# Splitting streamed weights with transfers and ScalarE instead of ScalarE and VectorE

## The chip, the cores and the metric

One core of one Trainium2 chip. The kernel is a two-layer decoder trunk on 512 tokens in float32. The metric is the device time of one execution in microseconds (us).

## The reference, cut to what matters

```python
D_MODEL = 1024; SEQ = 512; DEPTH = 2
A_WIDTH = 2048; B_WIDTH = 1536; D_FF = 3072

def mixer_a(h, w_in, v_gain, w_s, b_s, w_out):
    z = jax.nn.gelu(h @ w_in)                    # w_in: 1024 x 4096
    u, v = jnp.split(z, 2, axis=-1)
    v = rms_norm(v, v_gain)
    ...                                          # chunks of 128 tokens, 8 groups
    sv = jnp.einsum("gts,bcsgd->bctgd", ws, v) + ...
    return (u * sv) @ w_out                      # 2048 x 1024

def mixer_b(h, w_in, ...):
    g, xb = jnp.split(h @ w_in, 2, axis=-1)      # 1024 x 3072
    ...                                          # convolution, two gates of 6 x 256 x 256 each, a scan
    return (hs * gelu(g)) @ w_out                # 1536 x 1024

def conv_ffn(h, w_up, conv_w, conv_b, w_down):
    up = causal_dwconv(h @ w_up, conv_w, conv_b) # 1024 x 6144
    gate, val = jnp.split(up, 2, axis=-1)
    return (jax.nn.gelu(gate) * val) @ w_down    # 3072 x 1024

def reference(x, ...):
    for i in range(DEPTH):
        h = rms_norm(x, norm_mix[i])
        x = x + (mixer_a(h, ...) if i % 2 == 0 else mixer_b(h, ...))
        h = rms_norm(x, norm_ffn[i])
        x = x + conv_ffn(h, ...)
    return rms_norm(x, norm_final)
```

All weights are float32 in the chip's memory and are used once per execution.

## The kernel before, in words

**Products.** Activations lie with their features on the partitions and the 512 tokens along the free dimension. To keep float32 accuracy, every operand of a large product is held in two parts of type float32r, a rounded large part and a small part that is the remainder; `mm3` multiplies large by large, large by small and small by large, three matmuls of 512 columns.

**Chunks.** Weights arrive in chunks of 256 input features by 512 output features: 512 KB, 1024 values on each of 128 partitions. There are 230 of them that go through `load`; four more, at the very start, go through `first_chunk`. Each is used for 24 matmuls (2 halves of the input features x 4 blocks of outputs x 3), in the order of the program: `av` and `au` (the two halves of `a_w_in`), `aow` (`a_w_out`), `fu0` (`f_w_up` of layer 0, 12 blocks of 4 chunks), `fd0` (`f_w_down`, 24 chunks), `bx`, `bg` (`b_w_in`) with the six gate chunks `gw` between them, `bow`, `fu1`, `fd1`. The number after the letters is block and chunk: `fu052` is chunk 2 of block 5. The chunks of `f_w_up` take two transfers of 256 KB, one from the gate half and one from the value half; the others take one of 512 KB, and the gate chunks take two.

**The split.** `load` fetches a chunk from SP's queue into a `raw` tile. `split` makes the large part `hi` by a copy on ScalarE (L89) and the small part `lo` by a subtraction on VectorE (L90). The three tags `raw`, `hi`, `lo` of the pool `wp` have three buffers each, so a chunk can be fetched and split well ahead of its matmuls. Both instructions are given a high priority, which the scheduler uses when it writes down each engine's order; after that each engine works strictly through its own queue.

**Other work.** VectorE and ScalarE also scale the products, run the convolutions (`conv`), the activations and the split of the activations (`to_parts`). In mixer A, `gate_spatial` puts small matmuls (`sv`, L418 and L419) between the chunks of `au1` to `aow0`. GpSimd does a handful of small things: the power -1/2 of the norms (`rsqrt_mean`, L213), a mask, one power for the decay constants (L175).

Of the kernel before, what the change touches and what calls it, by code (L numbers as in the profile page):

```python
# [8 lines left out]
F32 = mybir.dt.float32  # L9
BF16 = mybir.dt.bfloat16  # L10
F32R = mybir.dt.float32r
AF = mybir.ActivationFunctionType
ALU = mybir.AluOpType

P = 128
S = 512
# [4 lines left out]
AG = 8  # L21
# [6 lines left out]
HIGH = 1000  # L28
LRU_C = 8.0

# Columns of the packed per-channel vectors.
_COLS = {}
_off = 0
for _name, _n in (
# [10 lines left out]
def trunk(ctx: ExitStack, tc: tile.TileContext, xT, vecs, a_w_in, a_w_sT, a_b_s, a_w_out,  # L45
          b_w_in, b_w_a, b_w_x, b_w_out, f_w_up, f_w_down, out):
    nc = tc.nc

    const = ctx.enter_context(tc.tile_pool(name="const", bufs=1))
    wp = ctx.enter_context(tc.tile_pool(name="wp", bufs=3))  # L50
    yp = ctx.enter_context(tc.tile_pool(name="yp", bufs=24))
    wk = ctx.enter_context(tc.tile_pool(name="wk", bufs=7))
    pp = ctx.enter_context(tc.tile_pool(name="pp", bufs=8, space=bass.MemoryType.PSUM))
# [4 lines left out]
    def work(name="w"):  # L58
        return wk.tile([P, S], F32, tag="w", name=name)
# [4 lines left out]
    def yhi(name="yh"):  # L64
        return yp.tile([P, S], F32R, tag="yh", name=name)
# [1 line left out]
    def ylo(name="yl"):  # L67
        return yp.tile([P, S], F32R, tag="yl", name=name)

    # Activations whose tables differ, in the order of the program.  # L70
    last_act = []

    def act_in_order(*args, **kw):
# [7 lines left out]
    def small(n, name):  # L81
        return const.tile([P, n], F32, name=name)

    # A chunk of a weight: 1024 values a partition, in two parts that add up to it exactly.
    def split(raw, shape, name):
        hi = wp.tile(shape, F32R, tag="hi", name=f"{name}h")
        lo = wp.tile(shape, F32R, tag="lo", name=f"{name}l")
        with tc.high_priority(HIGH):
            nc.scalar.copy(hi, raw)  # L89
            nc.vector.tensor_tensor(lo, raw, hi.bitcast(F32), op=ALU.subtract)  # L90
        return hi, lo

    def load(shape, parts, name):
        raw = wp.tile(shape, F32, tag="raw", name=f"{name}r")
        for sl, src in parts:
            nc.sync.dma_start(sl(raw), src)
        return split(raw, shape, name)

    def mm3(ps, w, x, first, last):
        (wh, wl), (xh, xl) = w, x  # L100
# [1 line left out]
        nc.tensor.matmul(ps, wh, xl, start=False, stop=False)  # L102
        nc.tensor.matmul(ps, wl, xh, start=False, stop=last)  # L103

    # Feature-major product: one PSUM tile for each of four blocks of 128 output features.
    def block(kt, loader, acts, name, hooks={}):
        pss = [psum(f"{name}{m}") for m in range(4)]
        for kc in range(kt // 2):
            hi, lo = loader(kc)
            last = kc == kt // 2 - 1  # L110
            order = [(k, m) for m in range(4) for k in range(2)] if last else [(k, m) for k in range(2) for m in range(4)]
            for k, m in order:
                kk = 2 * kc + k
                w = (hi[:, k, m * P:(m + 1) * P], lo[:, k, m * P:(m + 1) * P])
                mm3(pss[m], w, acts[kk], kk == 0, kk == kt - 1)
            for hook in hooks.get(kc, ()):
                hook()
        return pss

    def loader_of(w, col, name):  # L120
        v = w.rearrange("(k p) n -> p k n", p=P)

        def f(kc):
            return load([P, 2, 512], [(lambda t: t, v[:, 2 * kc:2 * kc + 2, col:col + 512])], f"{name}{kc}")
        return f

# [1 line left out]
    vt = const.tile([P, NV], F32, name="vt")  # L128
    xall = const.tile([P, KD, S], F32, name="xall")
    xs = [xall[:, k, :] for k in range(KD)]  # L130
# [6 lines left out]
    def load_x(k):  # L137
        nc.sync.dma_start(xs[k], xT[k * P:(k + 1) * P, :])

    # Keeps the tensor engine's clock up while the first loads are under way.  # L140
    warm = work("warm").bitcast(BF16)[:, 0:S]
    nc.vector.memset(warm, 0.0)
    wps = psum("warm")
# [13 lines left out]
    mhalf = small(NC, "mhalf")  # L157
    nc.gpsimd.memset(mhalf, -0.5)

    # log of the sigmoid, by log1p(u) = 2 atanh(u / (2 + u)) with u = exp(-|lambda|)  # L160
    lam = vt[:, _COLS["b_lambda"]:_COLS["b_lambda"] + NB]
    ebase = small(NB, "ebase")
    nabs = small(NB, "nabs")
# [1 line left out]
    u = small(NB, "lu")  # L165
# [20 lines left out]
        nc.vector.tensor_scalar(c8, u, -LRU_C, None, op0=ALU.mult)  # L186
        nc.vector.tensor_scalar(c4, u, LRU_C / 2, None, op0=ALU.mult)

# [1 line left out]
    acc = const.tile([P, S], F32, name="acc")  # L190
    rbc = const.tile([P, S], F32, name="rbc")
    rc = small(NC, "rc")
# [4 lines left out]
    def norm_input(k, gain, ts=slice(None)):  # L197
        nc.scalar.activation(xh[k][:, ts], xs[k][:, ts], AF.Copy, scale=gain)  # L198
        nc.vector.scalar_tensor_tensor(  # L199
            xl[k][:, ts], xs[k][:, ts], gain, xh[k][:, ts].bitcast(F32), op0=ALU.mult, op1=ALU.subtract)  # L200
# [11 lines left out]
        nc.vector.tensor_scalar(ms[:, 0:w], total, 1.0 / n, EPS, op0=ALU.mult, op1=ALU.add)  # L212
        nc.gpsimd.tensor_tensor(dst, ms[:, 0:w], mhalf[:, 0:w], op=ALU.pow)  # L213

    # The token's sum over the features, one token a partition.
    def norm_stat():
        ps = psum("st")
        for c in range(NC):
            nc.tensor.matmul(ps[:, c:c + 1], acc[:, c * P:(c + 1) * P], ones_f[:, 0:1], start=True, stop=True)
        rsqrt_mean(rc, ps[:, 0:NC], D)  # L220

    # The same scale along the free dimension, on all partitions.
    def norm_spread():
        nc.vector.tensor_copy(rch, rc)
        nc.vector.tensor_tensor(rcl, rc, rch.bitcast(F32), op=ALU.subtract)
        pb = psum("rb")
        for i, r in enumerate((rch, rcl)):
            dg = work_r("dg")
            nc.vector.tensor_tensor(
                dg.rearrange("p (c t) -> p c t", c=NC),  # L230
                ident.unsqueeze(1).broadcast_to([P, NC, P]),
                r.bitcast(F32).unsqueeze(2).broadcast_to([P, NC, P]), op=ALU.mult)
            nc.tensor.matmul(pb, ones, dg, start=i == 0, stop=i == 1)
        nc.scalar.copy(rbc, pb)
# [6 lines left out]
        nc.vector.tensor_tensor(l, src, h.bitcast(F32), op=ALU.subtract)  # L241
        return h, l

    # A product back to the model's width, added to x; the next norm's input follows.
    def project(kt, w, acts, gain_name, gain_off, name, hooks={}):
        for mb in range(2):
            pss = block(kt, loader_of(w, mb * 512, f"{name}w{mb}"), acts, f"{name}p{mb}", {} if mb else hooks)
            for m in range(4):
                k = 4 * mb + m
                nc.vector.tensor_tensor(xs[k], pss[m], xs[k], op=ALU.add)  # L250
                norm_input(k, col(gain_name, gain_off + k))
                square(k)

    # The last one, with the norm that ends the trunk. The last chunks of the second block go by halves
    # of the tokens, so that the first half leaves while the second is multiplied.
    def project_out(kt, w, acts, name):
        sq7 = work("sq7")
        hw = S // 2
# [67 lines left out]
    nc.vector.memset(tiny, 0.0)  # L326
    nc.scalar.activation(tiny, tiny, AF.Gelu_apprx_tanh)

# [1 line left out]
    vsum = small(NC * 4, "vsum")  # L330
    vparts = {}
    vraw = {}
    wv = a_w_in.rearrange("(k p) n -> p k n", p=P)

    def first_chunk(kc, src):
        raw, hi, lo = (wp.tile([P, 2, 512], dt, tag=t, name=f"av0{kc}{t}") for dt, t in ((F32, "raw"), (F32R, "hi"), (F32R, "lo")))
        for i in range(2):
            k = 2 * kc + i
            load_x(k)
            nc.sync.dma_start(raw[:, i], src[:, i])  # L340
            with tc.high_priority(HIGH):
                norm_input(k, g0[:, k:k + 1])
                nc.scalar.copy(hi[:, i], raw[:, i])
                nc.vector.tensor_tensor(lo[:, i], raw[:, i], hi[:, i].bitcast(F32), op=ALU.subtract)
        return hi, lo

    for fb in range(4):
        pss = [psum(f"v{c}") for c in range(NC)]
        for kc in range(KD // 2):
            c0 = AW + fb * 512  # L350
            if fb == 0:
                hi, lo = first_chunk(kc, wv[:, 2 * kc:2 * kc + 2, c0:c0 + 512])
            else:
                hi, lo = load([P, 2, 512], [(lambda t: t, wv[:, 2 * kc:2 * kc + 2, c0:c0 + 512])], f"av{fb}{kc}")
            if fb == 1 and kc == 2:
                norm_spread()
            last = kc == KD // 2 - 1
            order = [(k, c) for c in range(NC) for k in range(2)] if last else [(k, c) for k in range(2) for c in range(NC)]
# [13 lines left out]
        for c in range(NC):  # L372
            v = yp.tile([P, S], F32, tag="yl", name=f"vr{c}{fb}")
            nc.scalar.activation(v, pss[c], AF.Gelu_apprx_tanh, scale=rc[:, c:c + 1])
            junk = work("junk")
            i = c * 4 + fb
# [6 lines left out]
    for fb in range(4):  # L383
        for c in range(NC):
            v, sc = vraw[c, fb], rv[:, c:c + 1]
# [2 lines left out]
            nc.vector.scalar_tensor_tensor(l, v, sc, h.bitcast(F32), op0=ALU.mult, op1=ALU.subtract)  # L388
            vparts[c, fb] = (h, l)

    # The lower triangle of the spatial weights, [s, g, t]: s <= t stays.
    wsr = wp.tile([P, AG, P], F32, tag="raw", name="wsr")
    nc.sync.dma_start(wsr, a_w_sT.rearrange("g s t -> s g t"))
    wsparts = []
    for i in range(AG // 2):
# [4 lines left out]
        both = yhi(f"ws{i}").rearrange("p (g two t) -> p g two t", g=2, two=2)  # L400
# [4 lines left out]
    yparts = []  # L405
    uts = []

    # v's large part meets both parts of the weights side by side; the small products share one place.
    def gate_spatial(d):
        g = d // 2  # L410
        w = wsparts[g // 2][:, g % 2]
# [26 lines left out]
            uts.append(ut)  # L438
    project(AW // P, a_w_out, yparts, "norm_ffn", 0, "ao", spatial_hooks(3))

# [1 line left out]
    def conv(dst, src, taps, wname, cname, woff, wstep, coff):  # L442
        last = taps - 1
        nc.scalar.activation(dst, src, AF.Identity, scale=col(wname, woff + last * wstep), bias=col(cname, coff))  # L444
        for i in range(1, taps):
            nc.vector.scalar_tensor_tensor(  # L446
                dst[:, i:], src[:, :S - i], col(wname, woff + (last - i) * wstep), dst[:, i:],
                op0=ALU.mult, op1=ALU.add)
# [31 lines left out]
    conv_ffn(0, "norm_mix", KD)  # L480
    log_sigmoid()

# [1 line left out]
    xbparts = []  # L484
    gts = []

# [21 lines left out]
    rts, ths, its, hss = [], [], [], []  # L508

    gw = {}  # L510

    # r, tanh(-log_a / 2) and i * xb
    def gates(j):
        head, e = j // 2, j % 2
        if not e:
# [112 lines left out]
```

## Time and profile before

| | |
|---|---|
| median of 2 runs | 1341.85 us (1341.41 to 1342.29) |
| profiled execution, first to last instruction (span) | 1339.3 us |
| TensorE (PE) busy | 1329.0 us, 99% |
| VectorE (DVE) busy | 802.6 us, 60% |
| ScalarE (ACT) busy | 554.0 us, 41% |
| GpSimd (POOL) busy | 12.0 us, 1% |
| moved by transfers | 129.19 MB, mean 96 GB/s |

The profile records one execution. It gives no time of its own for that execution beside the span; the timed runs are 2.1 to 3.0 us longer than it, which is what lies around the first and the last instruction. A busy share is an average over stages, and matmuls are pipelined, so a busy PE says that matmuls followed each other closely and not that each ran at its best.

### The profile page before, as it was taken

How to read it: one execution, taken by the hardware profiler on the slowest of the kernel's cores; microseconds unless marked ns; L12 is line 12 of the kernel's file. 1: busy time of each engine (PE TensorE's matmuls, PEld its weight loads, DVE VectorE, ACT ScalarE, POOL GpSimd, SP SyncE). 2: the span in 40 equal slices, each digit the busy share in tenths (PEclk: the TensorE clock that was granted, in tenths of full speed). 3: DMA queues.
4: the chain of work that ended last, by engine and by line, in shares of the span. 5: the costliest groups of instructions: out<-in, count | busy, mean ns of one | idle time of the engine just before them, and what ended most of it. 6: DMA issues, size and time to landing. Idle time of an engine off the chain costs nothing.

```text
span 1339.3 us, 15007 instructions
## 1 busy us (share of the span) xinstructions
PE 1329.0 (99%) x5862; PEld 1082.5 (81%) x5862; DVE 802.6 (60%) x1104; ACT 554.0 (41%) x743; POOL 12.0 (1%) x20
## 2 busy tenths in 40 slices
PE   9999999999999999999999999999999999999997
PEld 7888888888888888888888888888888888888886
DVE  7227775446767575724247799944676757572325
ACT  6455332333434343423233669633343434342322
POOL 1000000000000000000000000000000000000000
PEclk9999999999999999999999999999999999999999
DMA  6333222232222222232233323232222222223221
GB/s 230 94 94 109 80 79 94 94 95 94 94 95 90 94 90 92 94 105 98 94 94 95 95 79 95 97 108 94 95 94 95 90 94 90 92 93 105 99 79 64
DMA packets 96328, 129.19 MB, mean 96 GB/s; under 512 B 5888, under 2 KB 61184, under 8 KB 96256
## 3 DMA queue, kind: packets, MB, share of 16 engines
q1 hardware_dynamic: 96112, 128.22, 29.7%
q8 instruction: 46, 0.75, 0.2%
q14 instruction: 26, 0.21, 0.1%
q10 hardware_dynamic: 144, 0.00, 0.0%
HBM read 126.11 MB, written 2.10 MB: 96 GB/s over the span
## 4 chain that ended last, share of the span: by engine, by line
PE 98%; issue 0%; DMA 0%; DVE 0%; ACT 0%; DVEq 0%; POOLq 0%; POOL 0%
PE f L101 13%; PE f L102 13%; PE f L103 13%; PE fd0p L102 3%; PE fd0p L103 3%; PE fd0p L101 3%; PE fd1p L101 3%; PE fd1p L102 3%; PE fd1p L103 3%; PE u L101 2%; PE v L362 2%; PE v L363 2%; PE u L103 2%; PE u L102 2%; PE v L364 2%; PE aop L101 2%
## 5 line engine op out<-in xcount | busy, mean ns | idle before, releaser
L446 DVE SCALAR_TENSOR_TENSOR cv<-up,vt,cv 128x511 f32<-128x511 f32 (+1 forms) x192 | 140.8, 745 | 22.2 <-ACT cv L444 21.3
L444 ACT ACTIVATE cv<-up,vt 128x512 f32<-128x512 f32 x96 | 77.7, 812 | 77.3 <-DVE up L468 77.3
L468 DVE TENSOR_TENSOR up<-f,rbc 128x512 f32<-128x512 f32 x96 | 65.4, 683 | 0.2 <-issue 0.2
L473 DVE TENSOR_TENSOR cv<-cv 128x512 f32<-128x512 f32 x48 | 33.0, 688 | 1.0
L472 ACT ACTIVATE cv<-cv 128x512 f32<-128x512 f32 x48 | 30.2, 629 | 5.5 <-DVE cv L446 3.3
L198 ACT ACTIVATE xh<-xall,vt 128x512 fp32r<-128x512 f32 x24 | 17.2, 719 | 23.8 <-DVE xall L250 23.8
L422 DVE SCALAR_TENSOR_TENSOR sv<-sv,vt,bs 128x256 f32<-128x256 f32 x32 | 14.9, 477 | 19.1 <-PE sv L419 19.1
L207 ACT ACTIVATE sq<-xall 128x512 f32<-128x512 f32 (+1 forms) x37 | 21.7, 586 | 9.8 <-DVE xall L262 9.8
L446 DVE SCALAR_TENSOR_TENSOR xb<-xr,vt,xb 128x511 f32<-128x511 f32 (+2 forms) x36 | 25.5, 744 | 0.1
L208 DVE TENSOR_TENSOR acc<-acc,sq 128x512 f32<-128x512 f32 (+1 forms) x37 | 23.8, 642 | 2.0 <-ACT sq L207 1.9
L199 DVE SCALAR_TENSOR_TENSOR xl<-xall,vt,xh 128x512 fp32r<-128x512 f32 x24 | 17.9, 748 | 5.2 <-ACT xh L198 4.8
L213 POOL TENSOR_TENSOR rc<-ms,mhalf 128x4 f32<-128x4 f32 (+1 forms) x6 | 5.4, 905 | 1233.5 <-DVE ms L212 1233.5
L418 PE MATMUL sv<-ws,vh 128*128 128x256 f32 x64 | 15.4, 324 | 0.0
L424 DVE SCALAR_TENSOR_TENSOR sv<-sv,vt 128x256 f32<-128x256 f32 x32 | 15.0, 480 | 0.4
L419 PE MATMUL sv<-ws,vl 128*128 128x128 f32 x64 | 14.2, 222 | 0.0
L559 DVE TENSOR_TENSOR_SCAN hs<-riyh,sq 128x512 f32<-128x512 f32 x12 | 14.0, 1205 | 0.0
L76 ACT ACT_TABLE_LOAD x10 | 12.8, 1283 | 0.1
L419 PEld LDWEIGHTS sv<-ws,vl 128*128 128x128 f32 x64 | 12.2, 191 | 0.5
L418 PEld LDWEIGHTS sv<-ws,vh 128*128 128x128 f32 x64 | 12.1, 188 | 0.5
L437 ACT ACTIVATE u<-u 128x512 f32<-128x512 f32 x16 | 9.4, 625 | 7.1 <-DVE u L436 7.1
L444 ACT ACTIVATE xb<-xr,vt 128x512 f32<-128x512 f32 x12 | 9.8, 814 | 6.1 <-DVE xr L492 6.1
L388 DVE SCALAR_TENSOR_TENSOR vl<-vr,rv,vh 128x512 fp32r<-128x512 f32 x16 | 10.9, 747 | 1.9 <-ACT vh L387 1.9
(2590 smaller groups left out, 4210.9 us busy)
## 6 DMA issues: line engine op xcount, KB each, us to landing
xall<-xT SPq DMA_DIRECT2D x8, 256.0 KB, 5.0
outT<-o SPq DMA_DIRECT2D x8, 256.0 KB, 2.4
av00raw<-a_w_in SPq DMA_DIRECT2D x2, 256.0 KB, 3.7
av01raw<-a_w_in SPq DMA_DIRECT2D x2, 256.0 KB, 4.9
av02raw<-a_w_in SPq DMA_DIRECT2D x2, 256.0 KB, 5.7
av03raw<-a_w_in SPq DMA_DIRECT2D x2, 256.0 KB, 5.2
bs<-a_b_s SPq DMA_DIRECT2D x1, 512.0 KB, 6.0
av10r<-a_w_in SPq DMA_DIRECT2D x1, 512.0 KB, 6.5
```

The source lines that it names most:

```text
L101: nc.tensor.matmul(ps, wh, xh, start=first, stop=False)
L102: nc.tensor.matmul(ps, wh, xl, start=False, stop=False)
L103: nc.tensor.matmul(ps, wl, xh, start=False, stop=last)
L362: nc.tensor.matmul(pss[c], xh[kk][:, ts], hi[:, k, :], start=kk == 0, stop=False)
L363: nc.tensor.matmul(pss[c], xh[kk][:, ts], lo[:, k, :], start=False, stop=False)
L364: nc.tensor.matmul(pss[c], xl[kk][:, ts], hi[:, k, :], start=False, stop=kk == KD - 1)
L418: nc.tensor.matmul(ps[:, i], vh[:, ds_], w, start=True, stop=False)
L444: nc.scalar.activation(dst, src, AF.Identity, scale=col(wname, woff + last * wstep), bias=col(cname, coff))
L446: nc.vector.scalar_tensor_tensor(dst[:, i:], src[:, :S - i], col(wname, woff + (last - i) * wstep), dst[:, i:], op0=ALU.mult, op1=ALU.add)
L468: nc.vector.tensor_tensor(upt, pss[2 * half + j], rbc, op=ALU.mult)
L472: nc.scalar.activation(ts[0], ts[0], AF.Gelu_apprx_tanh)
L473: nc.vector.tensor_tensor(ts[1], ts[0], ts[1], op=ALU.mult)
```

## The change

The tile `raw` is gone. GpSimd's queue starts a transfer that reads the float32 weight and writes float32r straight into `hi` (L90), so that the transfer rounds. ScalarE writes `-hi` into `lo` (L92). GpSimd's queue then starts a second transfer of the same weight that adds what it reads onto `lo` (L94). The weight is thus read from memory twice. `hi` and `lo` get four buffers each instead of three. `first_chunk` keeps its split on ScalarE and VectorE, from temporary tiles in another pool. The spatial weights keep a `raw` buffer of their own.

```diff
-    wp = ctx.enter_context(tc.tile_pool(name="wp", bufs=3))
+    wp = ctx.enter_context(tc.tile_pool(name="wp", bufs=4))
...
-    def split(raw, shape, name):
+    def load(shape, parts, name):
         hi = wp.tile(shape, F32R, tag="hi", name=f"{name}h")
         lo = wp.tile(shape, F32R, tag="lo", name=f"{name}l")
+        for sl, src in parts:
+            nc.gpsimd.dma_start(sl(hi), src)
         with tc.high_priority(HIGH):
-            nc.scalar.copy(hi, raw)
-            nc.vector.tensor_tensor(lo, raw, hi.bitcast(F32), op=ALU.subtract)
+            nc.scalar.activation(lo, hi.bitcast(F32), AF.Copy, scale=-1.0)
+        for sl, src in parts:
+            nc.gpsimd.dma_start(sl(lo), src, accum_op=ALU.add)
         return hi, lo
-
-    def load(shape, parts, name):
-        raw = wp.tile(shape, F32, tag="raw", name=f"{name}r")
-        for sl, src in parts:
-            nc.sync.dma_start(sl(raw), src)
-        return split(raw, shape, name)
...
     def first_chunk(kc, src):
-        raw, hi, lo = (wp.tile([P, 2, 512], dt, tag=t, name=f"av0{kc}{t}") for dt, t in ((F32, "raw"), (F32R, "hi"), (F32R, "lo")))
+        hi, lo = (wp.tile([P, 2, 512], F32R, tag=t, name=f"av0{kc}{t}") for t in ("hi", "lo"))
         for i in range(2):
             k = 2 * kc + i
+            raw = yp.tile([P, S], F32, tag="yl", name=f"av0{kc}raw{i}")
             load_x(k)
-            nc.sync.dma_start(raw[:, i], src[:, i])
+            nc.sync.dma_start(raw, src[:, i])
...
-    wsr = wp.tile([P, AG, P], F32, tag="raw", name="wsr")
+    wsr = wp.tile([P, AG, P], F32, tag="raw", name="wsr", bufs=1)
```

**Place 1: the last block of `au` and the start of `aow`.** Before, SP's queue holds one transfer for each chunk and nothing between them (`r` at the end of a name is the raw tile):

```order
L96 DMA au30r<-a_w_in 128x2x512
L96 DMA au31r<-a_w_in 128x2x512
L96 DMA au32r<-a_w_in 128x2x512
L96 DMA au33r<-a_w_in 128x2x512
L96 DMA aow00r<-a_w_out 128x2x512
L96 DMA aow01r<-a_w_out 128x2x512
```

Now GpSimd's queue holds, at the same place, the transfer into `hi` (`h`) and the adding transfer into `lo` (`l`) of each chunk in turn:

```order
L94 DMA au30l<-a_w_in 128x2x512
L90 DMA au31h<-a_w_in 128x2x512
L94 DMA au31l<-a_w_in 128x2x512
L90 DMA au32h<-a_w_in 128x2x512
L94 DMA au32l<-a_w_in 128x2x512
L90 DMA au33h<-a_w_in 128x2x512
L94 DMA au33l<-a_w_in 128x2x512
L90 DMA aow00h<-a_w_out 128x2x512
L94 DMA aow00l<-a_w_out 128x2x512
L90 DMA aow01h<-a_w_out 128x2x512
```

The loads moved from SP to GpSimd, and the queue alternates, so that a chunk's `h` stands behind the `l` of the chunk ahead of it, which waits for ScalarE's negation.

**Place 2: block 5 of `f_w_up`.** Before, SP's queue holds two transfers for each chunk ("x2"):

```order
L96 DMA fu050r<-f_w_up 128x2x256 x2
L96 DMA fu051r<-f_w_up 128x2x256 x2
L96 DMA fu052r<-f_w_up 128x2x256 x2
L96 DMA fu053r<-f_w_up 128x2x256 x2
L96 DMA fu060r<-f_w_up 128x2x256 x2
```

Now GpSimd's queue holds sixteen transfers for the block's four chunks:

```order
L90 DMA fu050h<-f_w_up 128x2x256 x2
L94 DMA fu050l<-f_w_up 128x2x256 x2
L90 DMA fu051h<-f_w_up 128x2x256 x2
L90 DMA fu052h<-f_w_up 128x2x256
L94 DMA fu051l<-f_w_up 128x2x256 x2
L90 DMA fu052h<-f_w_up 128x2x256
L90 DMA fu053h<-f_w_up 128x2x256 x2
L94 DMA fu052l<-f_w_up 128x2x256 x2
L94 DMA fu053l<-f_w_up 128x2x256 x2
```

The first two chunks go nearly one by one, and the last two go as a pair whose `h` transfers stand ahead of both `l`.

**Place 3: ScalarE in the same block.** Before, its queue holds the rounding copies among the convolutions of the block before (`cv`, `fy`):

```order
L89 CAST fu051h<-fu051r 128x1024
L444 ACTIVATE cv<-up,vt 128x512 x2
L89 CAST fu052h<-fu052r 128x1024
L472 ACTIVATE cv<-cv 128x512
L444 ACTIVATE cv<-up,vt 128x512
L240 CAST fy8h<-cv 128x512
```

Now the negations stand there in their place:

```order
L92 ACTIVATE fu050l<-fu050h 128x1024
L92 ACTIVATE fu051l<-fu051h 128x1024
L443 ACTIVATE cv<-up,vt 128x512
L471 ACTIVATE cv<-cv 128x512
L92 ACTIVATE fu052l<-fu052h 128x1024
L443 ACTIVATE cv<-up,vt 128x512 x3
```

One instruction of 128x1024 stands in ScalarE's queue for each chunk as before, but it is now in the middle of the chunk's way, between two transfers.

## Rows read from the trace of the kernel before

**Rows 1.** The page: span, and busy time of each engine

```profile
span 1339.3 us, 15007 instructions
PE 1329.0 (99%) x5862; PEld 1082.5 (81%) x5862; DVE 802.6 (60%) x1104; ACT 554.0 (41%) x743; POOL 12.0 (1%) x20
```

**Rows 2.** Waits of PE: line, releaser, us in total, times, longest

```profile
PE rb L285 <- DVE dg L278: 1.5, 1, 1.5
PE warm L145 <- DVE warm L142: 1.3, 1, 1.3
PE st L274 <- ACT sq L264: 1.0, 1, 1.0
PE v L362 <- ACT av00hi L343: 0.2, 1, 0.2
```

**Rows 3.** Weight loads on PE, order of time: first ones of two following chunks

```profile
503.28 0.19 PEld L101 LDWEIGHTS f<-xh,fu092h 128*128 128x128 f32 x1
...
508.90 0.19 PEld L101 LDWEIGHTS f<-xh,fu093h 128*128 128x128 f32 x1
```

**Rows 4.** One chunk's instructions: ns min/median/max, first and last start (us)

```profile
L101 PEld LDWEIGHTS f<-xh,fu0100h x8: 187/188/192, 514.5 to 519.4; 128*128 128x128 f32 x8
L89 ACT CAST fu0100h<-fu0100r x1: 1052/1052/1052, 503.5 to 503.5; 128x1024 fp32r<-128x1024 f32 x1
L90 DVE TENSOR_TENSOR fu0100l<-fu0100r,fu0100h x1: 1226/1226/1226, 504.6 to 504.6; 128x1024 fp32r<-128x1024 f32 x1
```

**Rows 5.** Stretches: length, busy PE, PEld, DVE, ACT, POOL; PE clock, DMA share, GB/s

```profile
96.00:186.00 90.00, 90.00 (x430) 74.36 (x429) 65.09 (x105) 40.62 (x62) 1.01 (x1) 1.00 0.28 91
...
280.00:550.00 270.00, 270.00 (x1160) 217.45 (x1159) 182.05 (x241) 113.24 (x145) 1.01 (x1) 1.00 0.29 94
...
1328.00:1339.30 11.30, 2.42 (x16) 1.72 (x14) 5.50 (x11) 1.12 (x3) 0.70 (x1) 0.71 0.54 186
```

**Rows 6.** The same view, whole span, line L90 alone (VectorE's subtractions)

```profile
0.00:1339.30 1339.30, 281.59 (x230) 1.00 0.30 96
```

**Rows 7.** Transfers by name: queue, KB each, median us from issue to landing

```profile
au22r<-a_w_in SPq DMA_DIRECT2D x1, 512.0 KB, 3.6
aow03r<-a_w_out SPq DMA_DIRECT2D x1, 512.0 KB, 3.5
...
fd0w05r<-f_w_down SPq DMA_DIRECT2D x1, 512.0 KB, 3.6
```

**Rows 8.** The issue of one of them on SP's queue, ns

```profile
L96 SPq DMA_DIRECT2D fd0w05r<-f_w_down x1: 368/368/368, 562.4 to 562.4; - x1
```

**Rows 9.** GpSimd's instructions by form: busy us, mean ns; idle before

```profile
L213 POOL TENSOR_TENSOR rc<-ms,mhalf 128x4 f32<-128x4 f32 x4 | 4.0, 1009 | 841.5 <-DVE ms L212 841.5
...
L175 POOL TENSOR_TENSOR lu<-ebase,nabs 128x12 f32<-128x12 f32 x1 | 2.3, 2279 | 18.6 <-DVE nabs L174 18.6
```

**Rows 10.** The page's costliest groups: the spatial matmuls

```profile
L418 PE MATMUL sv<-ws,vh 128*128 128x256 f32 x64 | 15.4, 324 | 0.0
L419 PE MATMUL sv<-ws,vl 128*128 128x128 f32 x64 | 14.2, 222 | 0.0
```

**Rows 11.** VectorE's groups by form: TENSOR_SCALAR on full tiles

```profile
L555 DVE TENSOR_SCALAR riyh<-riyh 128x512 f32<-128x512 f32 x12 | 4.7, 418 | 0.0
```

More of the change, by code (lines that the diff above doesn't have):

```diff
@@ L335, in first_chunk @@
     def first_chunk(kc, src):
-        raw, hi, lo = (wp.tile([P, 2, 512], dt, tag=t, name=f"av0{kc}{t}") for dt, t in ((F32, "raw"), (F32R, "hi"), (F32R, "lo")))
+        hi, lo = (wp.tile([P, 2, 512], F32R, tag=t, name=f"av0{kc}{t}") for t in ("hi", "lo"))
         for i in range(2):
             k = 2 * kc + i
+            raw = yp.tile([P, S], F32, tag="yl", name=f"av0{kc}raw{i}")
             load_x(k)
-            nc.sync.dma_start(raw[:, i], src[:, i])
+            nc.sync.dma_start(raw, src[:, i])
             with tc.high_priority(HIGH):
                 norm_input(k, g0[:, k:k + 1])
-                nc.scalar.copy(hi[:, i], raw[:, i])
-                nc.vector.tensor_tensor(lo[:, i], raw[:, i], hi[:, i].bitcast(F32), op=ALU.subtract)
+                nc.scalar.copy(hi[:, i], raw)
+                nc.vector.tensor_tensor(lo[:, i], raw, hi[:, i].bitcast(F32), op=ALU.subtract)
         return hi, lo
```

## The prediction

> **What bounds the kernel now.** I read the page's first lines, then the waits of TensorE (PE), then one chunk in order of time. PE is busy for 1329.0 of 1339.3 us [rows 1], and its waits come to 4 us in all, none of them for a streamed weight [rows 2]. So PE is the bound from the second stage to the tail, and the whole span has 10.3 us in it that is not PE. A chunk takes PE c = 5.62 us (the first weight load of one chunk at 503.28, of the next at 508.90, [rows 3]), 22.5 us for a block of four. The split is far ahead of it: chunk fu0100 is rounded at 503.5 and first multiplied at 514.5, 11 us later [rows 4]. VectorE's 281.6 us of subtractions [rows 6] lie on no path to the end. The transfer engines are busy for about 0.3 of each stage [rows 5]. The question is therefore not what the removed work gives, but whether the new way of a weight still keeps up with 5.62 us per chunk.
>
> **What is removed.** 230 subtractions at 1.2 us leave VectorE, and the SP transfers of the chunks go. The gain on the path is nothing; its upper end is what PE stands still now, 10.3 us or 0.8%, less than the 2% (27 us) that a measurement of this kernel can tell from no change. ScalarE trades a rounding copy of 1.05 us [rows 4] for a negation of the same size, which I price at the same 1.05.
>
> **What is added, and its prices.** A chunk now passes GpSimd's queue, the transfer engines, ScalarE, GpSimd's queue and the transfer engines again. In front of its own `l` each chunk waits for its negation, and GpSimd's queue is strictly in order: what stands behind such an `l` (the next `h`, or the next block's) waits too. This turnaround takes the place of SP's queue, where loads stood one behind another with only free buffers to wait for. Five prices:
>
> - b, the engines' time for 512 KB by a plain transfer: the stretch 96 to 186 us moved 91 GB/s at a share of 0.28 [rows 5], so 325 GB/s when busy, and 524,288 bytes take 1.6 us.
> - f, the rest of the landing: 3.6 us from issue to landing [rows 7], less 0.37 of issue [rows 8], less 1.6, is 1.6 us.
> - n, the negation: 1.05 us [rows 4], plus about 0.25. ScalarE is busy 113.24 of 270 us in the f_w_up stage [rows 5], so 0.42 of arrivals find it half way through an instruction of some 0.7 us, which is 0.15, and I give two handovers 0.1. n = 1.3.
> - g, GpSimd's time to issue one transfer. The trace has none. The low end is SP's 0.37 us for the same transfer [rows 8]; the high end is GpSimd's dearest instruction, 2.28 us for twelve columns [rows 9]. A gain is excluded, as any issue takes time there. I take 1.0, GpSimd's usual row for a tiny tile [rows 9], since an issue is also a small program on that engine.
> - a, the engines' time for 512 KB that is added onto SBUF. The trace has none either. Low end: as a plain transfer, 1.6 us. High end: three plain passes (read the weight, read the tile, write the tile), 4.8. I take two, a = 3.2, since two things are read for each one written.
>
> The Trainium skill, "DMA: Bandwidth & Descriptors" (SWDGE vs HWDGE vs iDMA), says that adding or casting transfers can be issued from GpSimd only, where software computes the descriptors; its specifications give a first byte after about 1 us there and 0.6 us from SP. By that page g would be some 0.4 above SP's row, 0.77; a smaller g of this size shortens the sum below by a quarter at most. No row here shows it.
>
> **The sum.** I write down when each step can happen, counting from the moment at which GpSimd has issued the `l` ahead. A transfer starts half way through its issue, and the engines do one after the other, in order.
>
> *One by one (place 1).* The `l` ahead began at -0.5 and keeps the engines until 2.7. The next `h`, issued by 1.0, runs from 2.7 to 4.3, has landed at 5.9, is negated at 7.2, and its `l` is issued at 8.2. That is g/2 + a + b + f + n, 8.2 us for a chunk that PE eats in 5.6. Seventeen chunks go so in a row, au20 to aow10: 17 x 2.6 = 44 us. Two things come off. Four buffers let a load start three chunks (16.9 us) before its use, and one chunk's way from its `h` to its landed `l` is about 12.5, so 4 us are swallowed once. And PE has other work there: the spatial matmuls, 15.4 + 14.2 = 29.6 us for 16 gates [rows 10], 12 of which lie among these chunks, 22 us. The term is 18 us.
>
> *A block of f_w_up (place 2).* Every half now takes a full issue, 0.8 us of the engines for `h` and 1.6 for `l`. The block ahead leaves the engines at 2.9. 0h is issued by 2, landed at 6.1, negated at 7.4; 0l is issued until 9.4 and 1h and half of 2h until 12.4. The engines reach 1h after 0l, at 11.1; it has landed at 14.3 and is negated at 15.6. 1l, the rest of 2h, and 3h are issued until 20.6. 2h has landed at 21.7, is negated at 23.0, and the four `l` of chunks 2 and 3 are issued until 27.0. The block takes 27.0 us against 22.5, and 24 blocks lose 24 x 4.5 = 108 us.
>
> *f_w_down.* By the order one single chunk and one pair follow each other here, 16 times. Worked in the same way, the single one takes 9.8 us and the pair 9.8, 19.6 for three chunks against 16.9: 16 x 2.7 = 43 us.
>
> *The other 69 chunks* (av, the rest of au and aow, bx, bg, gw, bow) have both patterns mixed. At the 0.9 us per chunk of f_w_down this is 62; the full buffers with which the first stage starts (16.9 us) and one refill take some 22 off. 40 us.
>
> At the start nothing is lost: the pieces of POOL's own work that now stand among the loads (the decay power at 20 us, the first norm at 29) hold back chunks av11 and av13, whose matmuls come 10 us later. The tail is as before. In sum 18 + 108 + 43 + 40 = 209 us, about 1339 + 209 for the span, and with the 2.5 us that the median of the runs lies above the span, **1550 us**. PE then works 84% of the time.
>
> **Rivals.** *It hides (13%).* If adding costs no more than a plain transfer, a = 1.6, the same steps give 6.6 us one by one, 22.6 for a block of f_w_up and 14.8 for three chunks of f_w_down. Only the first is over, 17 us in all, which the spatial matmuls cover, and the time is 1342 to 1350. For it: the engines are idle 0.7 of the time [rows 5]. Against it: an addition must also read the tile. The point of decision is a of about 2.2 us at g = 1.0. Then not slower, and with some of the 10.3 us of standing time gone even slightly faster, though not by 2%.
>
> *Adding is dearer (22%).* With a = 4.8 the engines alone need 6.4 us for each chunk, above c. A block of f_w_up takes 33.4 (+10.9, 262 us), f_w_down 7.3 more per three chunks (117), the rest at the same 2.4 per chunk 146 after 22 off, au and aow 17 x 4.2 - 26 = 45: 570 us, 1910 in all.
>
> *Issuing is the bound (14%).* With g = 2.0, near the high end, the sixteen issues of a f_w_up block take 32 us, and with the waits the block takes 35.4: 24 x 12.9 = 310. Place 1 gives 27, the other 117 chunks about 1.2 each less 22, 118: 455 us, 1800 in all.
>
> *VectorE holds GpSimd up (5%).* GpSimd's issue is slowed whenever VectorE works. VectorE keeps 802.6 - 281.6 = 521 us, 0.39 of the span [rows 1, 6]; g would be 1.0 / 0.61 = 1.64, and between the sums at 1.0 and 2.0 that is about 1710. The Trainium skill, "SBUF — State Buffer" (Who interferes with whom), has the rule behind this: VectorE and GpSimd share a pair of ports, and a VectorE instruction in a two-port mode (copies and tensor_scalar) locks out the writing of descriptors; it expects tensor_tensor not to. By the page's letter the cost here is small, since the only such full-tile group is twelve tensor_scalar of 0.42 us, 4.7 us in all [rows 11].
>
> *The clock falls (4%).* The granted clock is 1.00 in every stage and 0.71 in the last 11.3 us, where PE is busy for only 2.42 [rows 5]. No row lies between. If PE's waits let it fall to the lower level, 1.2 GHz, a chunk would take PE 11.2 us and PE would be the bound again; in f_w_up and at place 1 that is 113 x 5.6 = 633 in place of 126, 2060 in all.
>
> **How the numbers follow.** 40% for the forecast, by which I mean 1460 to 1640; 2% are left for what I have not thought of, a gain among them. The range reaches from 1350, where the hidden case ends, to 1900, which takes in slow issue and most of dear adding; what lies outside is the clock, the upper part of dear adding and the lower part of the hidden case, under 2 in 10. Slower by over 2% has all cases but the hidden one, 86%; within 2%, 13%; faster, 1%.
>
> **What would show it.** Right: PE waits for `lo` tiles by way of the `l` transfers in all stages after mixer A's first half, GpSimd's queue waits mainly for ScalarE's negation, ScalarE's negation for the `h` transfer; f_w_up blocks last about 27 us; the share of the engines goes to about 0.75; an `l` transfer lands later after its issue than an `h`. Step by step: the issue rows on POOL give g, the share of the engines over the bytes gives a, VectorE's busy time falls by some 280 us and the end does not follow. Wrong: if PE stays at 99%, a is small; if GpSimd's issues stand back to back, g is the bound; if the share of the engines is near 1, a is. The least certain number is a, then g.

## The result and the profile after

The changed kernel takes 1823.99 us (1821.42 to 1826.57, 2 runs), 1.359 times the kernel before (95% interval 1.355 to 1.364). It is slower by 482 us where 209 were forecast: the time lies inside the range, the direction was right, and the loss is 2.3 times the forecast one.

The page of the changed kernel: span, busy times, clock and transfers by slice, the queue of GpSimd's transfers, and the chain that ended last by engine.

```profile
span 1819.6 us, 15181 instructions
...
PE 1497.4 (82%) x5862; PEld 1153.3 (63%) x5862; DVE 536.2 (29%) x874; ACT 548.6 (30%) x743; POOL 661.1 (36%) x684
...
PEclk9999988989889998998989999989889899999998
DMA  7776556667667677676766777766667767767674
...
q0 software_dynamic: 180608, 241.21, 67.1%
...
DMA 36%; issue 27%; POOL 12%; PE 12%; ACT 9%; DVE 0%; ACTq 0%; POOLq 0%; DVEq 0%
```

Against [rows 1], VectorE's busy time fell by 266 us (281.6 us of subtractions were taken from it, [rows 6]), and the end moved the other way. No engine is near full: PE is at 82%, GpSimd at 36%, and the transfer engines have a share of 0.67. The chain that ended last is no longer PE but a round of transfer, GpSimd and ScalarE ("issue" in it is time in which an engine waited for nothing that the profile shows). A stage in which nothing is full and all are on the path is one in which steps follow one another that could lie side by side.

GpSimd's own waits in the changed kernel (what it waited for, us in total, times, longest):

```profile
POOL av12l L94 <- ACT av12l L92: 8.7, 1, 8.7
POOL bx00l L94 <- ACT bx00l L92: 8.6, 1, 8.6
POOL fd1w011l L94 <- ACT fd1w011l L92: 8.3, 1, 8.3
```

Some 185 such groups stand among the 200 longest, each an `l` that waits for its negation, and 8 for PE. PE in turn waits for the `l` transfers: 264 of its 315 us of waits. The longest of them in total:

```profile
PE f L101 <- DMA fu061l<-f_w_up: 4.7, 2, 3.3
```

The queue in order of time, at place 1 (start, length, instruction; idle before and what ended it):

```profile
246.59 1.19 POOL L94 DMA_DIRECT2D aow02l<-a_w_out  x1 [7.11 <-ACT aow02l L92]
247.33 1.21 POOL L90 DMA_DIRECT2D aow03h<-a_w_out  x1
255.43 1.19 POOL L94 DMA_DIRECT2D aow03l<-a_w_out  x1 [6.89 <-ACT aow03l L92]
```

The negation that the last row waited for had itself waited for the landing of its `h`:

```profile
254.07 1.06 ACT L92 ACTIVATE aow03l<-aow03h 128x1024 fp32r<-128x1024 f32 x1 [3.48 <-DMA aow03h<-a_w_out]
```

One `l` to the next is 8.84 us, for a chunk that PE eats in 5.62 [rows 3]. The two issues are 0.74 us apart; the rest is waiting. What the transfer engines do in that time, by stretches of 1 us (the last two numbers are their share and GB/s, the one before is the clock; the share adds up the times of packets, which can overlap, so it can read above 1):

```profile
247.00:248.00 1.00, 1.00 (x6) 0.75 (x4) 1.00 (x2) 0.00 (x0) 1.00 (x2) 1.00 0.00 0
248.00:249.00 1.00, 1.00 (x8) 0.75 (x6) 1.00 (x3) 0.78 (x2) 0.54 (x1) 1.00 0.39 63
249.00:250.00 1.00, 1.00 (x7) 0.91 (x7) 1.00 (x3) 1.00 (x3) 0.00 (x0) 1.00 0.80 106
...
252.00:253.00 1.00, 1.00 (x6) 0.82 (x5) 0.54 (x1) 0.00 (x0) 0.00 (x0) 1.00 1.12 352
253.00:254.00 1.00, 1.00 (x6) 0.83 (x5) 0.00 (x0) 0.00 (x0) 0.00 (x0) 1.00 0.30 94
254.00:255.00 1.00, 1.00 (x7) 0.84 (x6) 0.00 (x0) 0.93 (x1) 0.00 (x0) 1.00 0.00 0
```

They stand still until nearly 2 us after the `l` began to be issued, add for some 3 us at a low rate, run the plain `h` at 352 GB/s, and stand still again until the next `l`. The landing of the `h` takes 6.7 us from its issue, of the `l` 5.9, against 3.5 to 3.6 for SP's loads [rows 7]:

```profile
aow03h<-a_w_out POOLq DMA_DIRECT2D x1, 512.0 KB, 6.7
aow03l<-a_w_out POOLq DMA_DIRECT2D x1, 512.0 KB, 5.9
```

In f_w_up, first weight loads of block 1 and block 11 in the changed kernel (first and last start after the colon):

```profile
L99 PEld LDWEIGHTS f<-xh,fu010h x8: 186/188/192, 403.0 to 409.4; 128*128 128x128 f32 x8
L99 PEld LDWEIGHTS f<-xh,fu0110h x8: 187/188/192, 732.8 to 740.8; 128*128 128x128 f32 x8
```

Ten blocks take 329.8 us, 33.0 each. Before, the same two chunks began at 312.1 and 537.0, 22.5 each.

### The profile page after: what moved, and what is told of

Read it like the earlier page. It is cut to its first block, busy times and chain, and to the rows that moved or that the text cites. A ratio compares the mean times of both kernels' runs of the same rounds, so it can differ in the third digit from the quotient of the medians.

```text
span 1819.6 us, 15181 instructions
## 1 busy us (share of the span) xinstructions
PE 1497.4 (82%) x5862; PEld 1153.3 (63%) x5862; DVE 536.2 (29%) x874; ACT 548.6 (30%) x743; POOL 661.1 (36%) x684
## 3 DMA queue, kind: packets, MB, share of 16 engines
q0 software_dynamic: 180608, 241.21, 67.1%
## 4 chain that ended last, share of the span: by engine, by line
DMA 36%; issue 27%; POOL 12%; PE 12%; ACT 9%; DVE 0%; ACTq 0%; POOLq 0%; DVEq 0%
ACT cv L443 1%; PE fd0p L101 1%; PE fd0p L99 1%; PE fd0p L100 1%; PE fd1p L101 1%; PE u L99 1%; PE u L101 1%; DMA fu032h<-f_w_up 1%; PE u L100 1%; DMA fu001h<-f_w_up 1%; PE f L101 1%; PE fd1p L99 1%; PE fd1p L100 1%; PE f L100 1%; PE f L99 1%
## 5 line engine op out<-in xcount | busy, mean ns | idle before, releaser
L443 ACT ACTIVATE cv<-up,vt 128x512 f32<-128x512 f32 x96 | 72.7, 801 | 1.9 <-DVE up L467 1.9
L248 DVE TENSOR_TENSOR xall<-fd0p,xall 128x512 f32<-128x512 f32 x8 | 5.5, 687 | 130.4 <-PE fd0p L101 130.4
L445 DVE SCALAR_TENSOR_TENSOR xb<-xr,vt,xb 128x511 f32<-128x511 f32 (+2 forms) x36 | 25.6, 745 | 11.2 <-ACT xb L443 11.1
L260 DVE TENSOR_TENSOR xall<-fd1p,xall 128x256 f32<-128x256 f32 (+1 forms) x12 | 6.1, 512 | 68.8 <-PE fd1p L101 68.6
L248 DVE TENSOR_TENSOR xall<-aop,xall 128x512 f32<-128x512 f32 x8 | 5.4, 687 | 59.3 <-PE aop L101 59.3
L248 DVE TENSOR_TENSOR xall<-bop,xall 128x512 f32<-128x512 f32 x8 | 5.4, 686 | 54.6 <-PE bop L101 54.6
L535 DVE TENSOR_TENSOR riyl<-riyl,xbs 128x512 f32<-128x512 f32 x12 | 8.3, 690 | 38.0 <-ACT riyl L76 38.0
L418 PE MATMUL sv<-ws,vl 128*128 128x128 f32 x64 | 14.2, 222 | 0.0
```

What stands on the lines that cost most here:

```text
L445: nc.vector.scalar_tensor_tensor(dst[:, i:], src[:, :S - i], col(wname, woff + (last - i) * wstep), dst[:, i:], op0=ALU.mult, op1=ALU.add)
```

## The experiments

**Does the adding cost the time, or the order of steps around it?** Four kernels take the parts of a chunk's way away one by one. In `plain_l` the second transfer writes in place of adding:

```diff
-            nc.gpsimd.dma_start(sl(lo), src, accum_op=ALU.add)
+            nc.gpsimd.dma_start(sl(lo), src)
```

> The second transfer writes the weight over lo in place of adding it; its wait for the negation and the order of the queue stay. It leaves out the remainder, so the small products are not the reference's. Theory (turnaround: the engines' time of an l, the h behind it, the landing and the negation follow one another in GpSimd's queue): the one-by-one chunks fall from 9.0 to about 7.1 us, a block of f_w_up from 33 to about 23.5, in all about 1390 us. Rival (GpSimd's issuing is the bound): the block of f_w_up stays near 33 and the time near 1800.

Measured: 1468.7 us, ratio 1.0945 (1.0923 to 1.0967). Of the 482 us, 355 go with the adding; 127 are left, more than the 50 expected. A one-by-one chunk takes 6.8 us, a block of f_w_up 25.8 (ten blocks from 328.0 to 585.5).

In `two_plain` the negation goes as well, so that no `l` waits:

```diff
-            nc.scalar.activation(lo, hi.bitcast(F32), AF.Copy, scale=-1.0)
...
-            nc.gpsimd.dma_start(sl(lo), src, accum_op=ALU.add)
+            nc.gpsimd.dma_start(sl(lo), src)
```

> Two plain transfers for each chunk from GpSimd's queue and no negation, so lo holds the weight and not the remainder. Theory (turnaround): nothing waits between h and l, the loads run ahead, 1342 to 1355 us and PE at 99%. Rival (issuing on GpSimd is the bound): f_w_up, with four issues for each chunk, stays well above 22.5 us a block, over 1450 us in all.

Measured: 1342.21 us, ratio 1.0003 (0.9993 to 1.0013), PE at 99%. Two transfers for each of the 230 chunks, all issued by GpSimd, cost nothing that can be told from no change; issuing is not the bound.

`add_no_neg` keeps the adding and drops the negation alone:

```diff
-        lo = wp.tile(shape, F32R, tag="lo", name=f"{name}l")
+        lo = next_lo(shape)
...
-            nc.scalar.activation(lo, hi.bitcast(F32), AF.Copy, scale=-1.0)
```

> Adding stays and the negation goes: lo is one of four standing tiles, zeroed once, onto which the weights are added again and again, so that it does not hold the remainder. Theory (turnaround): without the wait in the middle the engines do 3.3 + 1.6 us for a chunk of 2 KB rows and 4.2 + 1.6 for f_w_up beside PE's 5.62, so only f_w_up is a little over: 1345 to 1420 us. Rival (adding transfers are too slow for the engines): the time stays above 1700.

Measured: 1343.92 us, ratio 1.0016 (1.0006 to 1.0026). This is the run that parts the two theories: with every adding transfer in place the loss is gone, so it is not the adding as such. Its page shows where the engines' work is then, beside PE:

```profile
PE 1327.5 (99%) x5862; PEld 1081.5 (81%) x5862; DVE 538.0 (40%) x878; ACT 324.4 (24%) x514; POOL 665.5 (50%) x684
...
q0 software_dynamic: 180608, 241.21, 93.5%
```

The transfer engines are now at 0.94 and PE at 99%. In the changed kernel the same bytes took them 0.67 of a longer span.

`sp_round` keeps both the negation and the adding, and takes the load of `hi` out of GpSimd's queue:

```diff
-            nc.gpsimd.dma_start(sl(hi), src)
+            nc.sync.dma_start(sl(raw), src)
         with tc.high_priority(HIGH):
+            nc.scalar.copy(hi, raw)
             nc.scalar.activation(lo, hi.bitcast(F32), AF.Copy, scale=-1.0)
```

> The weight is fetched by SP and rounded by ScalarE as in the kernel before, the negation and the adding transfer stay; three buffers each for raw, hi and lo. Nothing but adding transfers is left in GpSimd's queue, so that no load stands behind a wait. Theory (turnaround): as add_no_neg, 1345 to 1420 us, with ScalarE 240 us busier. Rival (adding transfers are too slow): above 1600. A second rival, that ScalarE's two instructions in a row for each chunk are late: 1420 to 1600 with PE waiting for hi.

Measured: 1349.59 us, ratio 1.006 (1.0043 to 1.0076). With loads that stand behind no wait, the adding split costs 8 us. This run also prices the adding by itself, since GpSimd's queue holds nothing else:

```profile
q0 software_dynamic: 90304, 120.61, 59.2%
q1 hardware_dynamic: 96112, 128.22, 28.8%
```

0.592 x 1347.1 us over 230 chunks is 3.47 us of packet time for 512 KB, with SP's loads on the same engines. I had taken 3.2.

**The rounding transfer alone.** `pool_round` fetches `hi` from GpSimd and `raw` from SP, and VectorE subtracts as before:

```diff
             nc.gpsimd.dma_start(sl(hi), src)
+            nc.sync.dma_start(sl(raw), src)
         with tc.high_priority(HIGH):
-            nc.scalar.activation(lo, hi.bitcast(F32), AF.Copy, scale=-1.0)
-        for sl, src in parts:
-            nc.gpsimd.dma_start(sl(lo), src, accum_op=ALU.add)
+            nc.vector.tensor_tensor(lo, raw, hi.bitcast(F32), op=ALU.subtract)
```

> One part alone: hi is rounded by a transfer from GpSimd, raw is fetched by SP, and VectorE subtracts as in the kernel before; no negation and no adding transfer, three buffers each. Theory: nothing in GpSimd's queue waits for another engine's work on the same chunk, PE stays at 99%, 1341 to 1350 us. Rival (a rounding transfer is slow in itself): over 1370.

Measured: 1344.04 us, ratio 1.0016 (1.0006 to 1.0026). The rounding transfer is as good as free here. Its queue had a share of 34.4% of 1342.5 us, 2.0 us for a chunk, where SP's plain load had 1.6.

**The order of the queue, and nothing else.** `ahead1` has every instruction of the changed kernel and writes GpSimd's queue so that the next chunk's load stands ahead of this chunk's adding transfer:

```diff
+    def load(shape, parts, name):
...
+        while len(started) < min(n + AHEAD + 1, len(plan)):
+            start()
+        hi = started[n]
...
+        for sl, src in parts:
+            queue(sl(lo), src, accum_op=ALU.add)
```

> The changed kernel with one thing moved: GpSimd's queue is written so that the load of the next chunk's hi stands ahead of the adding transfer of this one, everywhere. Every instruction of the changed kernel is there. Theory (turnaround): the engines, the landing and the negation of the next chunk now run beside the wait, 3.5 + 1.6 us of the engines' time are under PE's 5.62, and the time goes back to 1345 to 1365 us. Rival (the adding transfers or the double reading cost the time themselves): above 1600.

Measured: 1342.63 us, ratio 1.0007 (0.9998 to 1.0017). The whole loss is given back by the order of one queue. The page and GpSimd's queue in f_w_up:

```profile
PE 1330.2 (99%) x5862; PEld 1082.7 (81%) x5862; DVE 537.0 (40%) x874; ACT 551.4 (41%) x743; POOL 665.4 (50%) x684
...
q0 software_dynamic: 180608, 241.21, 94.2%
```

```profile
408.86 1.48 POOL L125 DMA_DIRECT2D fu060h<-f_w_up  x2 [1.65 <-PE f L156]
410.42 2.46 POOL L125 DMA_DIRECT2D fu053l<-f_w_up  x2
414.48 1.48 POOL L125 DMA_DIRECT2D fu061h<-f_w_up  x2 [1.60 <-PE f L156]
415.94 2.51 POOL L125 DMA_DIRECT2D fu060l<-f_w_up  x2
```

One chunk is 5.62 us here, GpSimd waits for PE to leave a buffer and no longer for ScalarE: when `fu060l` comes up at 415.94, its negation is done, though only 0.8 us before (at 415.13). The engines have 0.942 x 1341.4 / 230 = 5.49 us of packet time in each 5.62; since packets can overlap, this doesn't say how near the engines are to their limit.

`ahead2` looks two chunks ahead:

```diff
-AHEAD = 1
+AHEAD = 2
```

> As the one before, but two chunks ahead, still with four buffers. The load then waits for PE to leave the chunk two back, and the adding transfer behind it has only that chunk's successor, 5.6 us, to land in, where issue and landing take about 7. Theory (what stands behind a wait in GpSimd's queue pays for it): two chunks take 7 + 5.6 us in place of 11.2, 0.7 more for each, 1480 to 1520 us in all. If looking further ahead only helps: as the one before.

Measured: 1601.38 us, ratio 1.1934 (1.1869 to 1.1999), a loss of 260 us where 140 to 180 were expected. The wait that stands in front is now PE's:

```profile
513.24 1.48 POOL L125 DMA_DIRECT2D fu072h<-f_w_up  x2 [2.27 <-PE f L156]
514.70 2.52 POOL L125 DMA_DIRECT2D fu070l<-f_w_up  x2
```

Of GpSimd's 200 longest waits 195 are now for PE, so what waits in front is as expected. The size is so only in f_w_up, where a chunk takes 6.1 us (245.8 for ten blocks) against 6.3 expected. In f_w_down of layer 0 it takes 8.2 (196.6 for 24), 11.7 and 5.4 by turns. There the granted clock was 0.81 to 0.83 (650 to 800 us), with PE standing still for a fifth of the time, so the PE that the loads wait for was itself slower:

```profile
PEclk9999999999999999888799999999999999999998
```

How much of the loss is the clock, no run separates.

**Why a block of f_w_up took 33 us and not 27.** `one_piece` and `two_rows` fetch its chunks in rows of 2 KB, in one transfer or in two, and `pairs` leaves the transfers and writes the queue as two loads and then two adding transfers:

```diff
-                return load([P, 2, 2, 256], [
-                    (lambda t, h=h: t[:, :, h, :], wu[:, 2 * kc:2 * kc + 2, h, b * 256:(b + 1) * 256]) for h in range(2)
-                ], f"fu{l}{b}{kc}")
+                return load([P, 2, 512], [(lambda t: t, wflat[:, 2 * kc:2 * kc + 2, b * 512:(b + 1) * 512])], f"fu{l}{b}{kc}")
```

> The chunks of f_w_up are fetched by one transfer of 512 KB (rows of 2 KB) in place of two of 256 KB (rows of 1 KB); the columns read are 512 neighbours and not the gate and value halves that belong together, so the products are of other columns. Bytes, matmuls and waits are as in the changed kernel. If the two issues and the smaller pieces are what made a block of f_w_up 33 us, the block falls to four chunks at f_w_down's 7.1, 28.5 us, and the time to about 1715. If the size of the pieces does not matter: about 1820.

Measured: 1690.44 us, ratio 1.2597 (1.2557 to 1.2638); a block takes 28.2 us (392.5 to 674.0 for ten). It does not decide, because the scheduler wrote another order for the single transfers: chunks go alone and in pairs by turns, and GpSimd waits long for ScalarE five times in two blocks in place of six. `two_rows` changes this to two transfers again:

```diff
-                return load([P, 2, 512], [(lambda t: t, wflat[:, 2 * kc:2 * kc + 2, b * 512:(b + 1) * 512])], f"fu{l}{b}{kc}")
+                return load([P, 2, 512], [
+                    (lambda t, k=k: t[:, k], wflat[:, 2 * kc + k, b * 512:(b + 1) * 512]) for k in range(2)
+                ], f"fu{l}{b}{kc}")
```

> The chunks of f_w_up are fetched by two transfers of 256 KB as in the changed kernel, with GpSimd's queue in the same order, but in rows of 2 KB (128 rows a transfer) in place of 1 KB (256 rows); the columns are neighbours, so the products are of other columns. If the small rows made the block of f_w_up 33 us in place of the 27 that I had worked out: about 29 us a block and 1725 us. If it is the number of waits in the queue, three in each block, with their landing times: 32 to 33 us and 1790 to 1825.

Measured: 1781.42 us, ratio 1.328 (1.3241 to 1.3318), with the queue in the order of the changed kernel; 31.3 us a block (399.0 to 712.2). The small rows cost 1.7 us a block. `pairs` is made from `ahead1`:

```diff
-        while len(started) < min(n + AHEAD + 1, len(plan)):
+        while len(started) < min(n // 2 * 2 + 2, len(plan)):
             start()
```

> The changed kernel with GpSimd's queue written in pairs everywhere: both loads of two chunks, then both adding transfers. Rows of 1 KB and two transfers for each chunk of f_w_up stay. If the waits of the queue are what counts (two in a block of f_w_up in place of three, one for two chunks elsewhere): 28 to 29 us a block, 14 for a pair of the other chunks, 1630 to 1680 us. If f_w_up's pieces count: the block stays at 33 and the time is about 1750.

Measured: 1530.86 us, ratio 1.1412 (1.1379 to 1.1445). With rows of 1 KB and two transfers for each chunk a block takes 27.2 us (325.7 to 597.6); the waits count for more than the pieces. The hand-run of the prediction had the three waits too, so what it had wrong is the length of each. The total is lower than expected, because outside f_w_up pairs come closer to PE's pace: f_w_down of layer 0 took 144.6 us, 6.0 a chunk where I had written 7 (5.44 in the kernel before).

## Why the prediction went as it did

**The mechanism was right.** The prediction put the loss into the turnaround of GpSimd's queue, named the negation as its wait and the load behind it as what pays. `add_no_neg`, `sp_round` and `ahead1` each take that turnaround away in another manner, with all adding transfers kept, and each comes within 0.6% of the kernel before. The rival "adding is dearer" falls with `add_no_neg` and `ahead1`, "issuing is the bound" with `two_plain`. "It hides" describes the same transfers in another order, as `ahead1` shows. For "VectorE holds GpSimd up" no run shows any sign: in `ahead1` VectorE is as busy in us as in the changed kernel and nothing is late. The Trainium skill, "SBUF — State Buffer" (Who interferes with whom), expects no such lock from tensor_tensor, and the trace agrees; no run here tests the two-port modes. One sign did not come: an `l` lands no later after its issue than an `h` (5.9 us against 6.7 at place 1), because the `h` runs behind the `l`.

The clock fell part of the way, to a mean of 0.916. In block 5 it was 0.50 (1.2 GHz) from 537.0 to 543.5 us, after PE had stood still for 2 us waiting for weights (533.8 to 535.9):

```profile
542.00:542.50 0.50, 0.50 (x3) 0.40 (x2) 0.31 (x1) 0.16 (x1) 0.50 (x1) 0.50 0.00 0
```

GpSimd's queue hardly ever waited for PE, and the negations of this block for landings, so a slower PE did not lengthen the turnaround there. No run separates the clock's share; `ahead1` has it at 1.00 again without a change to PE's work.

**The failed step is the size of one turnaround**, in "A transfer starts half way through its issue, and the engines do one after the other", with the landing priced from SP's loads. Place 1, from one `l` to the next:

| piece of one turnaround | forecast, us | measured, us |
|---|---|---|
| from the issue of `l` to its first packets | 0.5 | about 1.9 |
| engines, `l` and then `h` | 3.2 + 1.6 | about 4.9 together |
| end of `h` to landing | 1.6 | about 0.7 |
| negation, until the next `l` is issued | 1.3 | 1.4 |
| sum | 8.2 | 8.84 |

A single chunk was thus only 0.6 us off, and partly by luck: two larger errors, 1.4 us too little at the start and 0.9 too much at the landing, partly cancel. From issue to first packet the traces show 1.0 us for a load from SP (aow03r, kernel before), 1.4 for a plain one from GpSimd (aow03l in `plain_l`) and 1.9 for an adding one. The forecast's landing, priced from SP's whole 3.6 us, already held most of SP's start, and 0.5 stood there for the start again. In f_w_up the three waits of a block were 2.3, 1.2 and 2.3 us off. GpSimd's rows of block 5 in the changed kernel, those at which it has just waited:

```profile
531.25 2.44 POOL L94 DMA_DIRECT2D fu050l<-f_w_up  x2 [6.55 <-ACT fu050l L92]
...
541.76 2.45 POOL L94 DMA_DIRECT2D fu051l<-f_w_up  x2 [5.85 <-ACT fu051l L92]
...
550.39 2.43 POOL L94 DMA_DIRECT2D fu052l<-f_w_up  x2 [3.98 <-ACT fu052l L92]
```

With the next block's first `l` at 564.08 these are 10.5, 8.6 and 13.7 us, where the hand-run had 8.2, 7.4 and 11.4. There the addition began 1.9 us after its issue and took 3.65 us (533.2 to about 536.85), and a load of two halves behind it landed 6.7 us after the issue of its second half; a load of GpSimd alone lands in 3.3 (`two_plain`). `plain_l` shows that over half of it is no matter of adding: 25.8 us against 22.6 worked out for a = 1.6. `two_rows` gives 1.7 us of the 6 to the small rows.

**What was multiplied.** The loss is the turnaround less PE's 5.62, so that an error of a tenth in the one is a quarter or more in the other. The blocks of f_w_up, 6 us off each, are the term missed by most; the covers that I subtracted were too large as well. By term, in us of span:

| term | forecast | measured |
|---|---|---|
| au20 to aow10 | 18 | 41.5 |
| 24 blocks of f_w_up | 108 | 258 |
| f_w_down, both layers | 43 | 85 |
| the rest | 40 | 95 |
| sum | 209 | 480 |

In the first, 22 us of cover came from adding up the busy times of two lines of spatial matmuls [rows 10]. Matmuls of the two lines overlap in the profile, so their busy times don't add: in the kernel before the 15.4 and 14.2 us together cover only 16.1. The twelve gates lengthened this stage there by 11.1 us (99.6 us in all, less 8 chunks at 5.62 and 8 of aow at 5.44). So 11 us of the 22 were not there, nor were the 4 that the buffers were to swallow; and 16 chunks at 8.82 are 53 us above PE's pace without the gates, where I had 44. In f_w_down three chunks took 21.4 us (170.9 for 24) where I had 19.6, and PE's own pace there is 5.44 a chunk and not the 5.62 of f_w_up that I used, so that three lost 5.0 us and not 2.7; the rest was priced by the same 2.7. The engines' share came out at 0.67 and not at 0.75: the work lies in a longer span.

**The prices.** Issuing was 0.74 us against 1.0; adding 3.47 against 3.2; the negation 1.06 as priced; a load's share of the engines 2.0 and not 1.6. The Trainium skill, "DMA: Bandwidth & Descriptors" (Specifications), puts the first byte of a GpSimd transfer 0.4 us later than SP's, at about 1 and 0.6 us. On the difference the traces agree, 1.4 us to the first packet against 1.0; both are 0.4 longer here, counted from the start of the issue. Landing was 4.0 us for aow03h in `two_plain` against 3.5 from SP [rows 7]. I had set this sentence beside the price of issuing. The time to the first packet was where it mattered.

## What to carry to other kernels

When a chunk passes the same in-order queue twice with another engine's work in between, the queue has a turnaround, and every load behind the second pass pays it. Compare that turnaround, start to first packet and landing included, with the bound's pace, and put the next chunk's first pass ahead of this one's second before anything else is changed. One ahead gave everything back here. Two ahead lost 260 us: then the load waited for a buffer in front of the addition, and the clock fell in f_w_down. A margin that is a small difference of two sums is no better known than the larger sum.

## What the hardware showed that I had not expected

The same bytes cost the transfer engines different packet times, by share of the span over what each queue moved: 3.1 us for each MB loaded by SP (0.297 x 1339.3 / 128.22, the kernel before), 3.8 by two plain rounding transfers from GpSimd (0.676 x 1340.4 / 241.21, `two_plain`), and 6.6 by adding ones (0.592 x 1347.1 / 120.61, `sp_round`). Whether the extra of the second is the rounding or GpSimd's descriptors was not tried apart. And engines at a share of 0.94 for a whole span did not slow the matmuls beside them: PE kept 99% in `add_no_neg` and `ahead1`.
